# Attention products over 4, 32 or 64 keys made with 128 contraction rows in the second layer

## The chip, the cores and the metric

The kernel runs on one core of one Trainium2 chip. The metric is the device time of one launch in microseconds. Before the change it is 934.2 us, the median of three runs (933.96 to 939.34).

## What is computed

One inference step of a two-layer decoder, for a prompt of 512 tokens and for 8 sample sequences of 4 new tokens each. Layer one is a state-space mixer. After it, keys and values (8 heads of 128) are made once; layer two, where the change lies, is attention over them with three dilation groups per head:

```python
WINDOWS = (128, 512, 2048); DILATIONS = (1, 4, 16)
def dilated_mixer(h, attend, biases, g_norm, w_in, w_out):
    u = rmsnorm(h, g_norm) @ w_in                       # 24 query heads and a gate
    for g in range(N_DIL_GROUPS):
        o, lse = attend(q[:, :, g], biases[g], DILATIONS[g], WINDOWS[g] // DILATIONS[g])
        ...
    w = softmax(stack(lses)); o = sum(w * stack(outs))  # groups weighted by their log-sum-exp
    return (o * silu(gate)) @ w_out
```

A prompt query attends causally to prompt keys at distances 0, d, 2d, ...; a sample query attends to the same pattern over a cache of 1024 older rows followed by its own 4 new rows. In both, the weights p = exp(score - max) multiply the values.

## The kernel before

All weights of the projections are split into a high and a low part (`whi`, `wlo`), so that a projection is three products per block. In layer two one core does three things interleaved on TensorE:

- the projections of layer two (tiles `pa`, `pb`), which run as a "filler": after each attention step the program puts 24 or 20 projection matmuls into the stream;
- `attend(h, n)`, the prompt attention of head h and query block n (0 to 3, 128 queries each). Queries and keys are ordered by residue class mod 4. The scores `sp` are one dense product for the window of 128 and, for the strided groups, products per residue class r that give w = 32(n+1) keys. `ptp` holds the transposed weights, which ScalarE copies to `pt`. `pv` is the output: one or two products of 128 keys, and then four products, one for each r, of 32 output columns with w rows of weights against `vr`, the values in strided order. w is 32, 64, 96 and 128 for n = 0, 1, 2, 3;
- `sample(h, q)`, the sample attention of head h and half q (4 sequences each): scores `s1`, `s2` against 640 cached keys (`kc`) and the 4 new ones, weights transposed (`w`) and copied to `wt`, and the output `so`: five products of 128 keys (`vc`) for each of 4 sequences, and a sixth of 4 keys (`vn`, the new values).

The order on TensorE is that of the written program. A loop over units (four `attend` and two `sample` per head, 49 units with one `combine` that joins the groups of the samples) calls at each turn one stage of each unit in flight and then the filler. A unit's stages are scores, transposes, output product, and (for `attend`) the transpose of the output. Loads go through SyncE's queue in program order: `kc`, `vc` and `vn` per sample unit, `kv` (a head's keys, values and, in four blocks of 32 partitions, the strided values) once per head, `wraw` (projection weights). `kc` and `vc` have two buffers each, one for each half of a unit's load.

In the profile all matmuls are recorded at line 146 (`mm`), transposes at line 149; each f32 matmul of these attention tiles shows as two records. "128\*32" behind a tile's name is rows by columns of the weights in the array. Loading weights into the array is a row of its own (PEld).

Of the kernel before, what the change touches and what calls it, by code (L numbers as in the profile page):

```python
# [12 lines left out]
F32 = mybir.dt.float32  # L13
# [8 lines left out]
TS = 4  # L22
# [12 lines left out]
ATH = 8  # L35
# [92 lines left out]
def tile_yoco_step(  # L128
# [6 lines left out]
    nc = tc.nc  # L135
    dma = nc.sync.dma_start
# [8 lines left out]
    def mm(*a, **k):  # L145
        pin(nc.tensor.matmul(*a, **k))  # L146
# [144 lines left out]
    vnd = dram.tile([NB, TS, ATH, 128], F32, name="vnd")  # L291
    kvd = dram.tile([ATH, 128, T + SEQ], F32, name="kvd")

    def dap(t, off, ap):
        a = t[:]
        return bass.AP(tensor=a.tensor, offset=a.offset + off, ap=ap)
# [3 lines left out]
    wk = actx.enter_context(tc.tile_pool(name="wk_a", bufs=2))  # L300
# [645 lines left out]
    wk = bctx.enter_context(tc.tile_pool(name="wk_b", bufs=2))  # L946
# [90 lines left out]
    for m in range(KD):  # L1037
        w = nxt
# [61 lines left out]
    for i, (f, h, wi) in enumerate(order):  # L1100
        w = [nxt]
# [63 lines left out]
    wk = bctx.enter_context(tc.tile_pool(name="wk_d", bufs=2))  # L1165
# [8 lines left out]
    y_s = wk.tile([128, ATH, NB * TS], F32, name="ys", bufs=1)  # L1174
    qpad = [wk.tile([128, NB, 32], F32, name=f"qpad{i}", bufs=1) for i in range(3)]
    sbt = wk.tile([128, SK], F32, name="sbt", bufs=1)
    for t_ in qpad + [sbt]:
        nc.gpsimd.memset(t_, 0.0)
    scale = 1.0 / math.sqrt(128.0)
    qp_t, kv_t = {}, {}  # L1180
# [186 lines left out]
    def attend(h, n):  # L1367
        bt, qp = bt_t[h], [qp_t[h, g] for g in range(3)]
        kv = kv_t[h]
        kt = kv[:, 0, :]  # L1370
        vb, vr = (kv[:, i, 0:SEQ].rearrange("p (n d) -> p n d", n=4) for i in (1, 2))
        kp = kt[:, NS:T]
        ktr = kp.rearrange("p (n r i) -> p r n i", n=4, r=4)
        bt12 = bt[:, 256:512].rearrange("p (a c) -> p a c", a=2)
        w = 32 * (n + 1)
        g0 = 128 if n == 0 else 256
        sp = pss("sp")
        k0 = max(0, n - 1) * 128
        for g in range(2):
            for r in range(4):  # L1380
                mm(sp[32 * r:32 * r + 32, g0 + w * g:g0 + w * g + w],
                   qp[1 + g][:, 128 * n + 32 * r:128 * n + 32 * r + 32], ktr[:, r, 0:n + 1, :], start=True, stop=True)
        mm(sp[:, 0:g0], qp[0][:, 128 * n:128 * n + 128], kp[:, k0:128 * n + 128], start=True, stop=True)
        s_ = wk.tile([128, 512], F32, name="s", bufs=3)
        mx = wk.tile([128, 4], F32, name="mx", bufs=4)
        s12 = s_[:, g0:g0 + 2 * w].rearrange("p (a c) -> p a c", a=2)
        nc.vector.tensor_tensor_reduce(out=s12, in0=sp[:, g0:g0 + 2 * w].rearrange("p (a c) -> p a c", a=2),
                                       in1=bt12[:, :, 128 - w:128], scale=1.0, scalar=-3e38,
                                       op0=ALU.add, op1=ALU.max, accum_out=mx[:, 1:2])
        nc.vector.tensor_tensor_reduce(out=s_[:, 0:g0], in0=sp[:, 0:g0], in1=bt[:, 256 - g0:256], scale=1.0,  # L1390
                                       scalar=-3e38, op0=ALU.add, op1=ALU.max, accum_out=mx[:, 0:1])
        nc.vector.tensor_scalar(mx[:, 2:3], mx[:, 0:1], mx[:, 1:2], -1.0, op0=ALU.max, op1=ALU.mult)
        nc.scalar.activation(s_[:, 0:g0 + 2 * w], s_[:, 0:g0 + 2 * w], AF.Exp, bias=mx[:, 2:3], accum_out=mx[:, 3:4])
        nc.vector.tensor_tensor(s12[:, 0, :], s12[:, 0, :], s12[:, 1, :], op=ALU.add)
        nc.vector.reciprocal(mx[:, 3:4], mx[:, 3:4])
        yield
        tp = pss("ptp", (128, 3, 128))
        nk = g0 // 128
        for i in range(nk):
            transpose(tp[:, i, :], s_[:, 128 * i:128 * i + 128], ident)  # L1400
        transpose(tp[0:w, 2, :], s_[:, g0:g0 + w], ident)
        pt = wk.tile([128, 3, 128], F32, name="pt", bufs=2)
        nc.scalar.copy(pt[:, 0:nk, :], tp[:, 0:nk, :])
        nc.scalar.copy(pt[0:w, 2, :], tp[0:w, 2, :])
        yield
        pv = pss("pv")[:, 0:128]
        for i in range(nk):
            b = n - nk + 1 + i
            mm(pv, pt[:, i, :], vb[:, b, :], start=i == 0, stop=False, skip_group_check=True)
        for r in range(4):  # L1410
            mm(pv[32 * r:32 * r + 32, :], pt[0:w, 2, 32 * r:32 * r + 32], vr[0:w, r, :],
               start=False, stop=True, skip_group_check=True)
        on = wk.tile([128, 128], F32, name="on", bufs=1)
        nc.scalar.activation(on, pv, AF.Copy, scale=mx[:, 3:4])
        yield
        if h not in op_t:
            op_t[h] = pss("op")
        op = op_t[h]
        transpose(op[:, 128 * n:128 * n + 128], on, ident)
        op_n[h] = op_n.get(h, 0) + 1  # L1420
        yt = y_t[h // 4][:, h % 4, :]
        if h == 7 and op_n[h] >= 3:
            c0, c1 = ((128, SEQ), (0, 128))[op_n[h] - 3]
            y7 = yt[:, NS + c0:NS + c1]
            assert len(gated) == 2
            nc.vector.scalar_tensor_tensor(y7, op[:, c0:c1], 0.5, y7, op0=ALU.mult, op1=ALU.mult)
            y_split(h, NS + c0, NS + c1)
        elif h < 7 and op_n[h] == 4:
            nc.vector.tensor_copy(yt[:, NS:T], op)
            att_done.add(h)  # L1430
# [5 lines left out]
    def sample(h, q):  # L1436
        if q == 0:
            sample_bias(h)
        qs = qpad[h % 3]
        kt = kv_t[h][:, 0, :]  # L1440
        s1, s2 = pss("s1"), pss("s2")
        kc = []
        for jp in range(2):
            kc.append(wk.tile([128, 2, NU], F32, name="kc", bufs=2))
            dma(kc[jp], ck[h, q, :, 2 * jp:2 * jp + 2, :])

        for o, c0, c1 in ((s1, 0, 512), (s2, 512, NU), (s2, NU, SK)):
            for j in range(4):
                b = 4 * q + j
                keys = kc[j // 2][:, j % 2, c0:c1] if c1 <= NU else kt[:, TS * b:TS * b + TS]  # L1450
                mm(o[32 * j:32 * j + 32, c0 % 512:c0 % 512 + c1 - c0], qs[:, b, :], keys, start=True, stop=True)
        ss = wk.tile([128, SK], F32, name="ss", bufs=1)
        mx = wk.tile([128, 4], F32, name="mxs", bufs=2)
        i16 = 2 * h + q
        nc.vector.tensor_tensor_reduce(out=ss[:, 0:512], in0=s1, in1=sbt[:, 0:512], scale=1.0, scalar=-3e38,
                                       op0=ALU.add, op1=ALU.max, accum_out=mx[:, 0:1])
        nc.vector.tensor_tensor_reduce(out=ss[:, 512:SK], in0=s2[:, 0:SK - 512], in1=sbt[:, 512:SK], scale=1.0,
                                       scalar=-3e38, op0=ALU.add, op1=ALU.max, accum_out=mx[:, 1:2])
        nc.vector.tensor_scalar(mx[:, 2:3], mx[:, 0:1], mx[:, 1:2], -1.0, op0=ALU.max, op1=ALU.mult)
        nc.scalar.activation(ss, ss, AF.Exp, bias=mx[:, 2:3], accum_out=lsm[:, i16:i16 + 1])  # L1460
        nc.gpsimd.tensor_copy(lse[:, i16:i16 + 1], mx[:, 2:3])
        nc.vector.reciprocal(mx[:, 3:4], lsm[:, i16:i16 + 1])
        vc = []
        for jp in range(2):
            vc.append(wk.tile([128, 2, 5, 128], F32, name="vc", bufs=2))
            dma(vc[jp], cv[h, q, :, 2 * jp:2 * jp + 2, :, :])
        yield
        vn = wk.tile([TS, 4, 128], F32, name="vn", bufs=1)
        dma(vn, dap(vnd, h * 128 + 4 * q * TS * ATH * 128, [[ATH * 128, TS], [TS * ATH * 128, 4], [1, 128]]))
        w1, w2 = pss("w1", (128, 4, 128)), pss("w2", (128, 2, 128))  # L1470
        for i in range(5):
            transpose((w1[:, i, :] if i < 4 else w2[:, 0, :]), ss[:, 128 * i:128 * i + 128], ident)
        transpose(w2[0:TS, 1, :], ss[:, NU:SK], ident)
        wt = wk.tile([128, 6, 128], F32, name="wt", bufs=1)
        nc.scalar.copy(wt[:, 0:4, :], w1)
        nc.scalar.copy(wt[:, 4, :], w2[:, 0, :])
        nc.scalar.copy(wt[0:TS, 5, :], w2[0:TS, 1, :])
        yield
        so = pss("so")[:, 0:128]
        for i in range(6):  # L1480
            for j in range(4):
                rows = slice(32 * j, 32 * j + 32)
                if i < 5:
                    mm(so[rows, :], wt[:, i, rows], vc[j // 2][:, j % 2, i, :], start=i == 0, stop=False, skip_group_check=True)
                else:
                    mm(so[rows, :], wt[0:TS, 5, rows], vn[:, j, :], start=False, stop=True, skip_group_check=True)
        nc.scalar.activation(o_s[:, q, h, :], so, AF.Copy, scale=mx[:, 3:4])

    def combine():
# [161 lines left out]
    for u in range(len(units) + LA + 2):  # L1651
        i = u - LA
# [5 lines left out]
        if u < len(units):  # L1658
            f, a = units[u]
# [104 lines left out]
```

## Time and profile before

| | us |
|---|---|
| median of three runs | 934.2 |
| the profiled execution | 930.12 |
| its span, first to last instruction | 928.3 |
| TensorE busy in the span | 912.0 (98%) |
| VectorE / ScalarE / GpSimd busy | 683.7 / 489.6 / 163.9 |
| granted TensorE clock, mean | 0.998 |

"Busy" of TensorE counts the time in which a matmul is under way, and its matmuls overlap, so short pauses between their starts do not show as idle time; they show in the starts and in the idle time of the weight loads. Layer two's attention runs from about 590 to 870 us.

### The profile page before, as it was taken

What the parts mean: (1) busy time and instruction counts of PE and PEld (TensorE: products, weight loads), DVE (VectorE), ACT (ScalarE), POOL (GpSimd) and SP (SyncE); (2) the same over time, 40 slices, a digit from 0 to 9 for tenths busy, and PEclk for the clock granted to TensorE, in tenths of its full rate; (3) what the DMA queues carried; (4) which work ended last, traced back from release to release, by engine and by line L of the source; (5) the groups of instructions that cost most, each with busy time, mean ns of one, the idle gap of its engine ahead of it and who ended that gap; (6) DMA issues with size and microseconds to landing.
All of it is one profiled execution on the core that took longest, in us unless ns stands there. A gap on an engine that the chain in (4) does not pass through costs nothing.

```text
span 928.3 us, 21878 instructions
## 1 busy us (share of the span) xinstructions
PE 912.0 (98%) x8671; PEld 842.9 (91%) x8671; DVE 683.7 (74%) x1435; ACT 489.6 (53%) x1140; POOL 163.9 (18%) x206
## 2 busy tenths in 40 slices
PE   8999999999999999999999999999999999999997
PEld 8989888988788889999999999988888888888997
DVE  6998899989799799555598346866677766777732
ACT  6678655755665655322255213555555555557642
POOL 2030344533433533111011000000000000000021
PEclk9999999999999999999999999999999999999999
DMA  8224365365357432546286555767867877784511
GB/s 296 92 74 158 97 212 188 122 200 159 127 171 233 138 132 96 159 137 209 84 285 204 190 177 181 255 208 250 279 192 250 265 228 255 258 267 144 191 49 49
DMA packets 80573, 168.48 MB, mean 182 GB/s; under 512 B 19990, under 2 KB 37736, under 8 KB 79960
## 3 DMA queue, kind: packets, MB, share of 16 engines
q1 hardware_dynamic: 73784, 154.60, 50.8%
q10 hardware_dynamic: 5616, 9.75, 2.8%
q0 software_dynamic: 1072, 2.74, 1.2%
q8 instruction: 68, 1.11, 0.5%
q14 instruction: 33, 0.27, 0.1%
HBM read 141.14 MB, written 25.93 MB: 180 GB/s over the span
## 4 chain that ended last, share of the span: by engine, by line
PE 82%; DVE 10%; ACT 2%; DMA 2%; issue 2%; POOL 0%; SPq 0%; ACTq 0%; POOLq 0%; DVEq 0%
PE pa L146 33%; PE pb L146 28%; PE sp L146 3%; PE so L146 3%; PE pv L146 2%; PE s L146 2%; DVE wlo L206 2%; DVE co L641 1%; PE yd L146 1%; DVE vl L874 1%; DMA m<-aed 1%; PE w L149 1%; PE ptp L149 1%; PE csp L146 1%; PE xp L149 1%
## 5 line engine op out<-in xcount | busy, mean ns | idle before, releaser
L205 ACT ACTIVATE whi<-wraw 128x1024 fp32r<-128x1024 f32 x69 | 72.9, 1056 | 95.7 <-PE pb L146 53.0
L206 DVE TENSOR_TENSOR wlo<-wraw,whi 128x1024 fp32r<-128x1024 f32 x69 | 88.8, 1287 | 46.9 <-ACT whi L205 46.4
L146 PE MATMUL pa<-bq,whi 128*128 128x272 f32 x512 | 103.1, 296 | 0.0
L146 PE MATMUL pb<-nl,whi 128*128 128x288 f32 x280 | 83.6, 298 | 0.0
L146 PE MATMUL pb<-nh,wlo 128*128 128x288 f32 x280 | 83.1, 297 | 0.0
L146 PE MATMUL pb<-nh,whi 128*128 128x288 f32 x280 | 83.0, 296 | 0.0
L146 PEld LDWEIGHTS pa<-bq,whi 128*128 128x128 f32 x512 | 81.2, 189 | 0.9
L146 PE MATMUL pa<-nh,whi 128*128 128x256 f32 x280 | 80.0, 286 | 0.0
L146 PE MATMUL pa<-nl,whi 128*128 128x256 f32 x280 | 79.7, 285 | 0.0
L146 PE MATMUL pa<-nh,wlo 128*128 128x256 f32 x280 | 79.1, 282 | 0.0
L146 PE MATMUL pb<-bq,whi 128*128 128x272 f32 x384 | 77.2, 296 | 1.2 <-DVE kv L1225 0.8
L146 PE MATMUL pa<-bq,wlo 128*128 128x272 f32 x256 | 74.2, 290 | 0.0
L641 DVE SCALAR_TENSOR_TENSOR co<-cb,cvp,co 128x568 f32<-128x568 f32 x72 | 65.4, 911 | 1.3 <-ACT co L639 0.7
L146 PEld LDWEIGHTS pb<-bq,whi 128*128 128x128 f32 x384 | 60.8, 189 | 2.5 <-DVE kv L1225 1.0
L1284 ACT ACTIVATE whi<-wraw 128x512 fp32r<-128x512 f32 x64 | 40.1, 627 | 36.4 <-PE pb L146 16.6
L146 PEld LDWEIGHTS pb<-nl,whi 128*128 128x128 f32 x280 | 52.5, 188 | 4.4 <-issue 4.4
L146 PE MATMUL pb<-bq,wlo 128*128 128x272 f32 x192 | 55.4, 289 | 0.0
L146 PEld LDWEIGHTS pb<-nh,wlo 128*128 128x128 f32 x280 | 52.7, 188 | 2.2 <-issue 2.2
L146 PEld LDWEIGHTS pa<-nh,whi 128*128 128x128 f32 x280 | 52.8, 189 | 1.9 <-issue 1.9
L146 PEld LDWEIGHTS pa<-nl,whi 128*128 128x128 f32 x280 | 52.7, 188 | 1.4 <-issue 1.4
L146 PEld LDWEIGHTS pa<-nh,wlo 128*128 128x128 f32 x280 | 52.7, 188 | 0.9 <-issue 0.9
L146 PEld LDWEIGHTS pb<-nh,whi 128*128 128x128 f32 x280 | 52.6, 188 | 0.8 <-issue 0.8
(403 smaller groups left out, 2779.7 us busy)
## 6 DMA issues: line engine op xcount, KB each, us to landing
wraw<-w_in SPq DMA_DIRECT2D x40, 512.0 KB
kc<-ck SPq DMA_DIRECT2D x32, 640.0 KB
vc<-cv SPq DMA_DIRECT2D x32, 640.0 KB
wraw<-wb SPq DMA_DIRECT2D x32, 512.0 KB
s<-s SPq DMA_DIRECT2D x32, 256.0 KB
m<-aed SPq DMA_DIRECT2D x16, 512.0 KB
ssmS<-s ACTq DMA_DIRECT2D x32, 256.0 KB
wraw<-w_out SPq DMA_DIRECT2D x16, 512.0 KB
```

Source lines behind the costliest of these rows:

```text
L146: pin(nc.tensor.matmul(*a, **k))
L149: pin(nc.tensor.transpose(*a))
L205: a = nc.scalar.activation(hi, raw, AF.Copy)
L206: b = lo_eng.tensor_tensor(lo, raw, f32(hi), op=ALU.subtract)
L641: nc.vector.scalar_tensor_tensor(o, cb[:, k:k + n], cvp[:, ti, k:k + 1], o, op0=ALU.mult, op1=ALU.add)
L874: nc.vector.scalar_tensor_tensor(v_l[g][:, i, :], v_t[g][:, i, :], gg, f32(v_h[g][:, i, :]), op0=ALU.mult, op1=ALU.subtract)
L1284: nc.scalar.activation(hi, src[p][j], AF.Copy)
```

## The change

Three persistent tiles replace tiles that were allocated per unit: `ptz` (four, one for each n, for the strided weights that were the third block of `pt`), `wt` and `vn`. GpSimd zeroes `vn`, the sixth block of `wt` and the four `ptz` once, ahead of layer two's attention. ScalarE and the load write the same few rows as before, and the products read all 128 rows, so the rest multiplies by zero. For the strided products the values read are all 128 partitions of `vr`, and so all four blocks of `kv`'s third part instead of the first n+1.

```diff
-    for t_ in qpad + [sbt]:
+    ptz = [wk.tile([128, 128], F32, name=f"ptz{i}", bufs=1) for i in range(4)]
+    wt = wk.tile([128, 6, 128], F32, name="wt", bufs=1)
+    vn = wk.tile([128, 4, 128], F32, name="vn", bufs=1)
+    for t_ in qpad + [sbt, vn, wt[:, 5, :]] + ptz:
         nc.gpsimd.memset(t_, 0.0)
...
-        pt = wk.tile([128, 3, 128], F32, name="pt", bufs=2)
+        pt = wk.tile([128, 2, 128], F32, name="pt", bufs=2)
         nc.scalar.copy(pt[:, 0:nk, :], tp[:, 0:nk, :])
-        nc.scalar.copy(pt[0:w, 2, :], tp[0:w, 2, :])
+        nc.scalar.copy(ptz[n][0:w, :], tp[0:w, 2, :])
...
         for r in range(4):
-            mm(pv[32 * r:32 * r + 32, :], pt[0:w, 2, 32 * r:32 * r + 32], vr[0:w, r, :],
+            mm(pv[32 * r:32 * r + 32, :], ptz[n][:, 32 * r:32 * r + 32], vr[:, r, :],
                start=False, stop=True, skip_group_check=True)
...
-        vn = wk.tile([TS, 4, 128], F32, name="vn", bufs=1)
-        dma(vn, dap(vnd, ...))
+        dma(vn[0:TS], dap(vnd, ...))
...
-                if i < 5:
-                    mm(so[rows, :], wt[:, i, rows], vc[j // 2][:, j % 2, i, :], start=i == 0, stop=False, ...)
-                else:
-                    mm(so[rows, :], wt[0:TS, 5, rows], vn[:, j, :], start=False, stop=True, ...)
+                vals = vc[j // 2][:, j % 2, i, :] if i < 5 else vn[:, j, :]
+                mm(so[rows, :], wt[:, i, rows], vals, start=i == 0, stop=i == 5, ...)
```

No instruction changes its place on TensorE, VectorE, ScalarE or SyncE; what changes are shapes, and a few waits. On TensorE, the output product of head 2's block n = 0, before, with the strided products (32 output columns each) behind one of 128 keys, and the scores `sp` of the next unit behind them:

```order
L149 MATMUL w_8517<-ident,ss 4x128
L146 MATMUL pv<-kv,pt 128x128 [waits PE_49]
L146 MATMUL pv<-kv,pt 32x128 [waits DMAHW1_49]
L146 MATMUL pv<-kv,pt 32x128 x3
L146 MATMUL sp<-kv,qp 32x96 [waits DVE_49,PE_49]
L146 MATMUL sp<-kv,qp 32x96 x7
L146 MATMUL sp<-kv,qp 128x256
```

The same place of the changed kernel:

```order
L149 MATMUL w_8520<-ident,ss 4x128
L146 MATMUL pv<-kv,pt 128x128 [waits PE_49]
L146 MATMUL pv<-kv,ptz_7035 32x128 [waits DMAHW3_49,DMAHW4_49,DMAHW2_49,DMAHW1_49]
L146 MATMUL pv<-kv,ptz_7035 32x128 x3
L146 MATMUL sp<-kv,qp 32x96 [waits DVE_49,PE_49]
L146 MATMUL sp<-kv,qp 32x96 x7
L146 MATMUL sp<-kv,qp 128x256
```

The strided products now wait for four loads, one per block of 32 partitions, where they waited for one. On GpSimd, the zeroing ahead of layer two's attention, before (`lse<-mxs` is its next work, in the sample units):

```order
L1178 MEMSET qpad_7032 128x256
L1178 MEMSET qpad_7033 128x256
L1178 MEMSET sbt 128x644
L1461 COPY lse<-mxs 128x1 [waits DVE_49] x16
L1629 TENSOR_TENSOR e<-e 128x272 [waits PE_49,Activation_49]
```

and in the changed kernel:

```order
L1182 MEMSET qpad_7032 128x256
L1182 MEMSET qpad_7033 128x256
L1182 MEMSET sbt 128x644
L1182 MEMSET vn 128x512
L1182 MEMSET wt 128x128
L1182 MEMSET ptz_7035 128x128
L1182 MEMSET ptz_7036 128x128
L1182 MEMSET ptz_7037 128x128
L1182 MEMSET ptz_7038 128x128
L1465 COPY lse<-mxs 128x1 [waits DVE_49] x16
```

Six zeroings are added behind the four that stood there; the copies behind them are the same.

More of the change, by code (lines that the diff above doesn't have):

```diff
@@ L1467, in sample @@
         yield
-        vn = wk.tile([TS, 4, 128], F32, name="vn", bufs=1)
-        dma(vn, dap(vnd, h * 128 + 4 * q * TS * ATH * 128, [[ATH * 128, TS], [TS * ATH * 128, 4], [1, 128]]))
+        dma(vn[0:TS], dap(vnd, h * 128 + 4 * q * TS * ATH * 128, [[ATH * 128, TS], [TS * ATH * 128, 4], [1, 128]]))
         w1, w2 = pss("w1", (128, 4, 128)), pss("w2", (128, 2, 128))
@@ L1473, in sample @@
         transpose(w2[0:TS, 1, :], ss[:, NU:SK], ident)
-        wt = wk.tile([128, 6, 128], F32, name="wt", bufs=1)
         nc.scalar.copy(wt[:, 0:4, :], w1)
@@ L1482, in sample @@
                 rows = slice(32 * j, 32 * j + 32)
-                if i < 5:
-                    mm(so[rows, :], wt[:, i, rows], vc[j // 2][:, j % 2, i, :], start=i == 0, stop=False, skip_group_check=True)
-                else:
-                    mm(so[rows, :], wt[0:TS, 5, rows], vn[:, j, :], start=False, stop=True, skip_group_check=True)
+                vals = vc[j // 2][:, j % 2, i, :] if i < 5 else vn[:, j, :]
+                mm(so[rows, :], wt[:, i, rows], vals, start=i == 0, stop=i == 5, skip_group_check=True)
         nc.scalar.activation(o_s[:, q, h, :], so, AF.Copy, scale=mx[:, 3:4])
```

## The prediction

> **What bounds the kernel now.** I read the page's busy times and chain first, then three stretches by engine, then who waits for whom in the stretch of the change. From the page:
>
> ```profile
> PE 912.0 (98%) x8671; PEld 842.9 (91%) x8671; DVE 683.7 (74%) x1435; ACT 489.6 (53%) x1140; POOL 163.9 (18%) x206
> PE 82%; DVE 10%; ACT 2%; DMA 2%; issue 2%; POOL 0%; SPq 0%; ACTq 0%; POOLq 0%; DVEq 0%
> ```
>
> TensorE is 82% of the chain that ended last. The stretch from 590 to 860 us (busy us of TensorE, its weight loads, VectorE, ScalarE, GpSimd; clock, DMA share, GB/s), and the waits of TensorE and of its weight loads there (us in total, times, longest):
>
> ```profile
> 590.00:860.00 270.00, 269.25 (x3422) 236.14 (x3421) 193.84 (x602) 152.03 (x410) 4.59 (x16) 1.00 0.72 237
> PE pb L146 <- DVE kv L1225: 0.8, 1, 0.8
> PEld s L146 <- issue: 5.9, 22, 0.3
> PEld s L146 <- PE so L146: 5.4, 21, 0.3
> PEld sp L146 <- issue: 4.8, 24, 0.2
> PEld so L146 <- issue: 4.4, 23, 0.2
> PEld s L146 <- DMA kc<-ck: 1.3, 2, 0.7
> ```
>
> Of 270 us, TensorE's matmuls cover 269.25, and one wait, of 0.8 us, is put down to another engine; VectorE has 193.84 us of work there and ScalarE 152.03. The stretch is as long as TensorE's stream, so time taken out of that stream leaves the total unless something else is then late. But the weight loads pause: 4.4 us ahead of `so`, 4.8 ahead of `sp`, 11.3 ahead of `s`, nearly all in pauses of 0.2 to 0.3 us and most under "issue", where no engine is to be seen as the cause. These pauses decide what the change is worth.
>
> **Few rows are no shorter and no longer by themselves.** Groups by shape:
>
> ```profile
> L146 PE MATMUL so<-vc,wt 128*32 128x128 f32 x640 | 20.8, 275 | 0.0
> L146 PE MATMUL so<-vn,wt 4*32 4x128 f32 x128 | 6.7, 280 | 0.0
> L146 PE MATMUL pv<-kv,pt 96*32 96x128 f32 x64 | 3.4, 285 | 0.0
> L146 PE MATMUL pv<-kv,pt 64*32 64x128 f32 x64 | 3.4, 281 | 0.0
> L146 PE MATMUL pv<-kv,pt 32*32 32x128 f32 x64 | 3.4, 280 | 0.0
> ```
>
> A product with 4 rows takes 280 ns, one with 128 takes 275. What differs is when they start. The first sample's output, from four views of single moments and short windows (starts of the first instruction of each group):
>
> ```profile
> 606.46 0.51 PE L146 MATMUL so<-vc,wt 128*32 128x128 f32 x12
> ...
> 606.68 0.29 PE L146 MATMUL so<-vc,wt 128*32 128x128 f32 x3
> 606.90 0.42 PE L146 MATMUL so<-vn,wt 4*32 4x128 f32 x8
> 607.25 0.64 PE L146 MATMUL s<-kc,qpad 128*32 128x512 f32 x4
> ...
> 607.70 0.61 PE L146 MATMUL s<-kc,qpad 128*32 128x512 f32 x4
> 608.13 0.40 PE L146 MATMUL s<-kc,qpad 128*32 128x128 f32 x8
> ```
>
> Matmuls come in bursts of four, one for each group of 32 columns. In `so<-vc` the bursts at 606.46 (twelve records, three bursts) to 606.68 are (606.68 - 606.46)/2 = 0.11 apart. From the last of them to the 4-row group it is 0.22, its two bursts and the way out take 607.25 - 606.90 = 0.35, and the first step of the scores is 0.45 where the second is 0.43. Weight loads at the same kind of place, for the strided products of n = 0, n = 1 and n = 2:
>
> ```profile
> 702.24 0.57 PEld L146 LDWEIGHTS pv<-kv,pt 128*128 128x128 f32 x10
> 703.02 0.32 PEld L146 LDWEIGHTS sp<-kv,qp 128*32 128x32 f32 x16 [0.20 <-issue]
> ...
> 748.43 0.27 PEld L146 LDWEIGHTS sp<-kv,qp 128*32 128x32 f32 x12 [0.20 <-issue]
> ...
> 719.50 0.80 PEld L146 LDWEIGHTS pv<-kv,pt 128*128 128x128 f32 x12
> 720.29 0.64 PEld L146 LDWEIGHTS sp<-kv,qp 128*32 128x32 f32 x18
> ```
>
> Behind 32 rows (702 us) and 64 rows (748 us) the loads of `sp` pause 0.20 us; behind 96 rows (719 us) they do not. So the pause goes with row counts up to 64, on the way in (from 128 rows) and on the way out, and 96 rows count as 128. The Trainium skill, "TensorE: Matmul & The Clock Gate", section "Why this matters for your kernels", says that a single product over 32 rows takes the same time as one over 128; by that rule alone padding would be worth nothing. The durations here agree (280 against 275 ns), the starts do not (0.22 against 0.11 us).
>
> **The change part by part.** I take a step of a padded group to be as in `so<-vc`, 0.11 us.
>
> (1) `so`, 16 times. From 606.68 to 607.25 are three steps, 0.57 us; padded 3 x 0.11 = 0.33. Saved 0.24, and 0.02 at the scores' first step: 0.26. 16 x 0.26 = 4.2 us. Fourteen of the 16 are followed by scores `s`, two by `sp`, which I price alike. If the steps stayed at the 0.13 that a first step after a pause has (0.35 - 0.22), it would be 0.57 - 0.39 = 0.18, or 2.9 us.
>
> (2) `pv` of n = 0 and n = 1. The same scores (three key blocks) follow once 32 rows, once 128:
>
> ```profile
> 702.35 0.74 PE L146 MATMUL pv<-kv,pt 128*128 128x128 f32 x10
> 703.02 1.17 PE L146 MATMUL sp<-kv,qp 128*32 128x96 f32 x18
> 703.83 0.48 PE L146 MATMUL pa<-bq,whi 128*128 128x272 f32 x1
> ...
> 833.45 0.97 PE L146 MATMUL pv<-kv,pt 128*128 128x128 f32 x12
> 834.23 1.14 PE L146 MATMUL sp<-kv,qp 128*32 128x96 f32 x18
> 835.02 0.48 PE L146 MATMUL pb<-bq,whi 128*128 128x272 f32 x1
> ```
>
> 32 rows: 703.83 - 702.35 = 1.48 us. 128 rows: 1.57, but with two more records of 128 keys at 0.11 each, so 1.35 like for like. Saved 0.13 (0.11 at the way out alone: 0.67 - (0.78 - 0.22)). Eight blocks n = 1 and seven n = 0: 15 x 0.13 = 2.0 us, at least 15 x 0.11 = 1.7. The eighth n = 0 is the last unit; projections of full width follow it, I count nothing. n = 2 (96 rows) and n = 3 save nothing. The way in stays: from 128\*128 to 32 columns it is the same with 128 rows (the sum of the 833 us rows holds it).
>
> (3) Six zeroings on GpSimd:
>
> ```profile
> 570.42 0.81 POOL L1178 MEMSET qpad<- 128x256 f32 x3 [68.19 <-DVE wlo L1285]
> 571.17 0.64 POOL L1178 MEMSET sbt<- 128x644 f32 x1
> 593.77 0.19 POOL L1461 COPY lse<-mxs 128x1 f32<-128x1 f32 x1 [21.96 <-DVE mxs L1459]
> ```
>
> 644 columns take 0.64 us, so 512 + 5 x 128 = 1152 take about 1.2. GpSimd then idles 21.96 us; the first `vn` load is issued at 588 us, the first `wt` copy runs at 600. Nothing is charged; without that cover it would be 1.2 us once.
>
> (4) The wider reads wait for four `kv` loads instead of one or two at the head of n = 0 and n = 1. Where the lead is shortest, head 6:
>
> ```profile
> 771.83 3.15 SPq L1187 DMA_DIRECT2D kv<-kvd x4
> ...
> 803.45 0.74 PE L146 MATMUL pv<-kv,pt 128*128 128x128 f32 x10
> ```
>
> The last of the four is issued by 775.0, 28.5 us ahead. Nothing, from either side; a wait would queue the whole of TensorE behind it, since it works in order. Weight loads with 128 rows take some ns more (`so<-vc` 106 to 110 against 101 to 104) beside running matmuls: nothing.
>
> Sum: 4.2 + 2.0 = 6.2 us, with bounds 2.9 + 1.7 = 4.6 and, with the unrounded last digits upward (0.27 and 0.14), 6.4.
>
> **What is late next.** The cache loads `kc`. Twice, the scores stood for them:
>
> ```profile
> 651.84 0.83 SPq L1445 DMA_DIRECT2D kc<-ck x2
> ...
> 658.66 0.23 PEld L146 LDWEIGHTS s<-kc,qpad 128*32 128x32 f32 x7 [0.65 <-DMA kc<-ck]
> ...
> 718.84 0.83 SPq L1445 DMA_DIRECT2D kc<-ck x2
> ...
> 726.06 0.16 PEld L146 LDWEIGHTS s<-kc,qpad 128*32 128x32 f32 x8 [0.20 <-PE so L146]
> ```
>
> A lead of 657.87 - 651.84 = 6.0 us is too short, 7.2 us is enough. A round of one sample (some 17 us) shrinks by 0.26 + 0.13 = 0.4 us; a load whose issue does not move with TensorE loses as much lead. Six of 16 leads are between 5 and 7.5 us, so at most 6 x 0.4 = 2.4 us come back. Since the issues wait for buffers that TensorE frees, they move along with it, and I charge 0.3.
>
> **Rivals.**
>
> *The pause is not from the rows* (the change does not do what it is built on). For it: the wait list puts 21 pauses ahead of `s` down to `so`, as if the scores waited for that product to end; then those stay, and at the least nothing is saved: 934.2. Against: the same 0.20 stands ahead of `sp` behind 32 and 64 rows under "issue", and not behind 96.
>
> *Taken back by `kc`.* Gain 6.2 - 2.4 = 3.8: 930.4. For it the two waits above, against it that issues follow TensorE.
>
> *Slower: every score step waits for `kc`.* If leads fell under 6 us in all 16 samples and each cost the 0.7 us seen at worst, that is 16 x 0.7 - 1.3 = 9.9 us, more than the 6.2: 937.9. It decides where the leads, mostly 7 to 14 us, lose over a microsecond; 0.4 is not that.
>
> *The first steps stay slow*: the lower bound 4.6, so 929.6.
>
> **How the numbers follow.** The profiled execution took 930.12 us with a span of 928.3; the sum is made in its time, which is 4.1 under the median of the runs (934.2), and I take the difference off the median. Forecast 934.2 - 6.2 + 0.3 = 928.3. Chances: the forecast, within a microsecond and a half, 0.68; the slow first steps or `kc` in part (930 to 932) 0.18; no gain 0.08; `kc` everywhere 0.03; more than the sum 0.03. The range takes the upper bound of the sum and some 3 us of spread (934.2 - 6.4 - 2.8; single executions lie 4.1 under the median and 5.1 over it) and the partial cases: 925.0 to 932.5. One per cent, about what can be told from no change here, is 9.3 us: faster by that would be under 924.9, above every term, 0.05; slower 0.03; within 0.92.
>
> **What would show it.** Right: no pause of the loads between `so<-vc`, `so<-vn` and `s`; 0.33 us from the last `so<-vc` burst to the scores; `sp` behind n = 0 and 1 without a pause; 590 to 860 us of before done in some 264. Wrong: the pauses of 0.20 with 128 rows in every shape; more or longer waits of `s` for `kc`; the wait for `DVE kv` (0.8) grown by what TensorE gained; a new wait of `pv` for loads of `kv`.

## The result

The changed kernel takes 930.19 us, the median of six runs (928.57 to 931.42), against 934.71 us for the kernel before, measured beside it. The ratio is 0.9942, with a 95% interval of 0.992 to 0.9964: a gain of 4.5 us by the medians and of 5.4 by the ratio (3.4 to 7.5), clear of the spread and within one per cent. Forecast were 928.3 us, a gain of 5.9.

The page of the profile after, its busy times and chain; the stretch from 590 to 860 us; and the waits from 593 to 862 us:

```profile
PE 910.9 (98%) x8671; PEld 849.9 (92%) x8671; DVE 683.4 (74%) x1435; ACT 489.8 (53%) x1140; POOL 162.2 (17%) x212
PE 82%; DVE 9%; DMA 4%; ACT 3%; issue 2%; POOL 0%; SPq 0%; POOLq 0%; DVEq 0%; ACTq 0%
...
590.00:860.00 270.00, 267.78 (x3469) 242.85 (x3469) 196.73 (x614) 155.22 (x414) 4.59 (x16) 1.00 0.73 243
...
PE pb L146 <- DVE kv L1229: 1.1, 1, 1.1
PEld s L146 <- DMA kc<-ck: 2.4, 2, 1.5
PEld s L146 <- issue: 5.1, 17, 0.3
PEld s L146 <- PE so L146: 3.9, 13, 0.3
PEld sp L146 <- issue: 1.8, 9, 0.2
PEld so L146 <- issue: 1.6, 9, 0.2
```

Two things are to be seen. The short pauses of the weight loads shrank: `sp` from 4.8 to 1.8 us, `so` from 4.4 to 1.6, `s` from 11.3 to 9.0. Those left of `so` stand where the columns go from 128 to 32, those left of `sp` nearly all where they go back from 32 to 128, and those left of `s` between its own steps; the change touches none of these. And the waits grew: for `kc` from 1.3 to 2.4 us, for `DVE kv` (a tile that VectorE writes) from 0.8 to 1.1. The first sample's output, matmul starts and weight loads:

```profile
610.10 0.73 PE L146 MATMUL so<-vc,wt 128*32 128x128 f32 x20
610.64 0.40 PE L146 MATMUL so<-vn,wt 128*32 128x128 f32 x8
610.86 1.15 PE L146 MATMUL s<-kc,qpad 128*32 128x512 f32 x12
...
610.53 0.24 PEld L146 LDWEIGHTS so<-vn,wt 128*32 128x32 f32 x8
610.75 0.24 PEld L146 LDWEIGHTS s<-kc,qpad 128*32 128x32 f32 x8
...
704.45 0.16 PEld L146 LDWEIGHTS pv<-kv,ptz 128*32 128x32 f32 x8
704.59 0.73 PEld L146 LDWEIGHTS sp<-kv,qp 128*32 128x32 f32 x17
```

Twenty records of `so<-vc` (five bursts) take 0.54, so 0.11 each, and the two padded bursts 610.86 - 610.64 = 0.22 where they took 0.35; the loads run through without a pause, also from `pv` of n = 0 to `sp`. The durations of one product hardly changed (273 ns where the 4 rows took 280):

```profile
L146 PE MATMUL pv<-kv,ptz 128*32 128x128 f32 x256 | 13.6, 285 | 0.0
L146 PE MATMUL so<-vn,wt 128*32 128x128 f32 x128 | 6.4, 273 | 0.0
```

The spans of the two profiles, 928.3 and 928.1 us, do not show the gain, because single executions differ by several us ahead of the change. So I compare stretches. From the first scores to the first product of the joining of the samples (`oc`), before and after:

```profile
591.24 0.64 PE L146 MATMUL s<-kc,qpad 128*32 128x512 f32 x4
861.23 0.29 PE L146 MATMUL oc<-sbt,os 128*128 128x16 f32 x2
```

```profile
595.22 0.64 PE L146 MATMUL s<-kc,qpad 128*32 128x512 f32 x4
860.83 0.29 PE L146 MATMUL oc<-sbt,os 128*128 128x16 f32 x2
```

269.99 us became 265.61: 4.4 us, which agrees with the runs. The work ahead of the first scores, which is the same, took 4.0 us more in this execution; its granted clock was 0.98 and 0.99 in the first two stretches of 200 us, where it was 1.00 before. From 590 to 860 us it was 1.00 in both. What is left to explain is a forecast of 6.2 us taken out of TensorE's stream and 4.4 found.

### The profile page after: what moved, and what is told of

The parts are those of the page before. It is cut to its first block, busy times and chain, and to the rows that moved or that the text cites. A ratio compares the mean times of both kernels' runs of the same rounds, so it can differ in the third digit from the quotient of the medians.

```text
span 928.1 us, 21890 instructions
## 1 busy us (share of the span) xinstructions
PE 910.9 (98%) x8671; PEld 849.9 (92%) x8671; DVE 683.4 (74%) x1435; ACT 489.8 (53%) x1140; POOL 162.2 (17%) x212
## 4 chain that ended last, share of the span: by engine, by line
PE 82%; DVE 9%; DMA 4%; ACT 3%; issue 2%; POOL 0%; SPq 0%; POOLq 0%; DVEq 0%; ACTq 0%
PE pa L146 33%; PE pb L146 28%; PE sp L146 3%; PE so L146 2%; PE pv L146 2%; PE s L146 2%; DMA m<-aed 2%; DVE co L641 2%; DVE wlo L206 1%; PE yd L146 1%; PE csp L146 1%; PE w L149 1%; PE ptp L149 1%; PE xp L149 1%; DVE v L703 1%
```

## The experiments

### One part at a time

The first keeps the padding of the samples' new values and gives the strided products their 32, 64 and 96 rows back, the second the other way round.

```diff
-            mm(pv[...], ptz[n][:, 32 * r:32 * r + 32], vr[:, r, :], ...)
+            mm(pv[...], pt[0:w, 2, 32 * r:32 * r + 32], vr[0:w, r, :], ...)      # first
...
-                vals = vc[j // 2][:, j % 2, i, :] if i < 5 else vn[:, j, :]   # second
-                mm(so[rows, :], wt[:, i, rows], vals, ...)
+                if i < 5:
+                    mm(so[rows, :], wt[:, i, rows], vc[j // 2][:, j % 2, i, :], ...)
+                else:
+                    mm(so[rows, :], wt[0:TS, 5, rows], vn[0:TS, j, :], ...)
```

> The new values of the samples padded to 128 rows, the strided products left at 32, 64, 96 rows. Theory (TensorE pauses when its row count goes past 64 in either direction): the step from so<-vc to so<-vn falls from 202 to 89 ns and from there to the scores from 197 to 89, 16 times, while sp behind n = 0 and n = 1 still comes 197 to 199 ns late. About two thirds of the stream's gain, 16 x 0.27 = 4.3 us, before any waits for loads; total some 930 to 931. Rival (the pause ahead of the scores is a wait for so to end): that step stays at 197, gain at most 2.2 us.

> The strided products padded, the new values of the samples read with 4 rows again. Theory: sp behind n = 0 and n = 1 comes at 89 ns, so<-vn keeps its 202 and 197 ns; gain 15 x 0.13 = 2.0 us, total some 932 to 933. Rival (the padded products cost something of their own, or the wider reads wait for kv): gain near 0 or less, and a wait of pv for loads of kv in the trace.

Ratios to the kernel before: 0.9969 (0.9949 to 0.9989) for the new values alone, 0.9979 (0.996 to 0.9997) for the strided products alone; 931.58 and 932.37 us against 934.98. The first is a little above the 930 to 931 that was expected: its profile lists 3.4 us of waits for `kc`, and its stretch from the first scores to `oc` is only 1.5 us shorter than before (the second's, with 1.5 us of such waits, 1.9). Such figures do not separate 2 us from 4, but a part of the trace without these waits does. A head's two rounds, the second head's first scores to the third's, hold no wait but the constant ones; first the kernel before, then the changed one, then the two parts (each from a view of the 0.35 us around these starts):

```profile
624.17 0.64 PE L146 MATMUL s<-kc,qpad 128*32 128x512 f32 x4
657.87 0.62 PE L146 MATMUL s<-kc,qpad 128*32 128x512 f32 x2
```

```profile
627.39 0.61 PE L146 MATMUL s<-kc,qpad 128*32 128x512 f32 x4
660.27 0.60 PE L146 MATMUL s<-kc,qpad 128*32 128x512 f32 x2
```

```profile
627.13 0.61 PE L146 MATMUL s<-kc,qpad 128*32 128x512 f32 x4
660.28 0.60 PE L146 MATMUL s<-kc,qpad 128*32 128x512 f32 x2
```

```profile
628.14 0.64 PE L146 MATMUL s<-kc,qpad 128*32 128x512 f32 x4
661.59 0.62 PE L146 MATMUL s<-kc,qpad 128*32 128x512 f32 x2
```

33.70 us before, 32.88 after, 33.15 with the new values alone, 33.45 with the strided products alone. The new values save 0.55 per head, 0.27 a sample; the strided products 0.25, 0.13 a block; together 0.82. The fourth, fifth and sixth heads repeat the first two of these figures within 0.01 us. Both parts do what the forecast said, they add up (0.80 against 0.82), and the rival that the pause ahead of the scores is a wait for `so` to end is out: it went with the rows alone.

### Which row counts

The third kernel pads the new values to 64 rows (and leaves the strided products padded to 128), the fourth pads everything to 96.

```diff
-                vals = vc[j // 2][:, j % 2, i, :] if i < 5 else vn[:, j, :]
-                mm(so[rows, :], wt[:, i, rows], vals, ...)
+                r_ = 128 if i < 5 else 64      # third; fourth: 96, and ptz[n][0:max(w, 96)], vr[0:max(w, 96)]
+                vals = vc[j // 2][:, j % 2, i, :] if i < 5 else vn[0:r_, j, :]
+                mm(so[rows, :], wt[0:r_, i, rows], vals, ...)
```

> As the changed kernel, but the new values of the samples padded to 64 rows only. Theory (it is the class of the row count, 96 and 128 being one class, 32 and 64 others): the two steps are 202 and 197 ns again, the stream 16 x 0.27 = 4.3 us longer than with 128 rows. Rival (4 rows are special, or padding helps by itself, or the new place of vn and wt in memory does it): the steps stay at 89 ns and the time at that of the changed kernel.

> As the changed kernel, but all padding goes to 96 rows instead of 128 (new values, and the strided products of n = 0 and n = 1). Theory: 96 counts as 128, every step at 89 ns, the time that of the changed kernel within the runs' spread. Rival (only equal row counts run through without a pause): steps of about 200 ns at so<-vn and behind pv, some 6 us more than the changed kernel.

With 64 rows, the head and its way out:

```profile
626.49 0.42 PE L146 MATMUL so<-vn,wt 64*32 64x128 f32 x8
626.85 0.64 PE L146 MATMUL s<-kc,qpad 128*32 128x512 f32 x4
660.29 0.62 PE L146 MATMUL s<-kc,qpad 128*32 128x512 f32 x2
```

With 96:

```profile
627.88 0.40 PE L146 MATMUL so<-vn,wt 96*32 96x128 f32 x8
628.10 0.61 PE L146 MATMUL s<-kc,qpad 128*32 128x512 f32 x4
661.00 0.60 PE L146 MATMUL s<-kc,qpad 128*32 128x512 f32 x2
```

64 rows give 0.36 from group to scores and a head of 33.44 us, as if the new values had 4 rows (33.45); 96 rows give 0.22 and 32.90, as 128 does (32.88). The ratios lean the same way, though their intervals overlap: 0.9978 (0.9962 to 0.9995) and 0.9955 (0.9938 to 0.9973). The zeroed tiles and their place in memory are the same in both, so they are not it. The Trainium skill, "TensorEngine Tiling (Array Packing)", section "Key Properties", says that a change of tiling mode drains the engine; its section "Available Configurations" names modes of 32, 64 and 128 rows. The runs agree as far as they go: they show no drain as such, only later starts, some 0.11 us at each crossing between 64 rows or fewer and 96 or more, and with the slower step behind it 0.13 to 0.15 in all. A crossing between 32 and 64 rows was not tried.

### One crossing instead of two

Four rows again, but as the first of the six products: `for i in (5, 0, 1, 2, 3, 4)`, with `start` and `stop` moved.

> As the changed kernel, but the new values of the samples have 4 rows again and come first of the six products instead of last. The way from the transposes to 32 columns costs 202 ns in any case, so theory: the 4-row group follows the transposes at 202, the first so<-vc follows it at about 197, and the scores follow the last so<-vc at 89; one pause instead of two, so the stream is 16 x 0.13 = 2.1 us longer than in the changed kernel. Rival (4-row products cost by themselves, wherever they stand): both steps about 200 ns, 4.3 us longer.

```profile
627.92 0.61 PE L146 MATMUL s<-kc,qpad 128*32 128x512 f32 x4
661.09 0.60 PE L146 MATMUL s<-kc,qpad 128*32 128x512 f32 x2
```

33.17 us a head, 0.29 more than in the changed kernel: 0.15 a sample, one crossing where 4 rows at the end cost two (0.27). Expected was 0.13. The ratio is 0.9949 (0.9934 to 0.9965), not to be told from the changed kernel: it had fewer waits for `kc` (1.3 us in four). So the cost is not in the four-row products themselves but in where they stand.

### Where the rest of the gain went: loads of cached keys

In the changed kernel the weight loads of the scores stand here:

```profile
661.27 0.23 PEld L146 LDWEIGHTS s<-kc,qpad 128*32 128x32 f32 x7 [0.88 <-DMA kc<-ck]
...
820.99 0.17 PEld L146 LDWEIGHTS s<-kc,qpad 128*32 128x32 f32 x4 [0.80 <-PE pv L146]
822.68 0.16 PEld L146 LDWEIGHTS s<-kc,qpad 128*32 128x32 f32 x8 [1.51 <-DMA kc<-ck]
```

The first and third are the places that waited before, by 0.65 and 0.67 us; the pause of 0.80, which the profile puts down to another product, and the 1.51 behind it are one unit, head 7's first. The loads of its keys were issued here, before and after, and between them those of head 2 after (heads count from 0):

```profile
814.75 2.38 SPq L1445 DMA_DIRECT2D kc<-ck  x2
...
654.59 0.83 SPq L1449 DMA_DIRECT2D kc<-ck  x2
...
814.32 2.58 SPq L1449 DMA_DIRECT2D kc<-ck  x2
```

Counted from each execution's first scores (591.24 and 595.22), head 2's loads were issued 1.2 us earlier than before, its scores began 1.6 us earlier. Head 7's loads were issued 4.4 us earlier, but TensorE was there 5.3 us earlier (at 820.19, where the pause of 0.80 begins, against 821.53 before). So the leads, from issue to scores, fell from 6.0 to 5.7 us and from 6.8 to 5.9: the issues moved along only in part. At head 7 they waited for other things than TensorE: the bias loads ahead of them 1.8 us for VectorE in both kernels, and the second load of keys 1.6 us for a load of values before and 1.8 after.

I tried to take these waits away twice by issuing the loads earlier. One kernel loads the next unit's keys right behind this unit's values:

```diff
+        nxt = (h, 1) if q == 0 else (h + 1, 0)      # behind the loads of vc
+        if nxt[0] < ATH:
+            kc_t[nxt] = load_kc(*nxt)
```

> The changed kernel, to be compared with the next on one chip: 0.994 of the kernel before, 929 to 931 us; two score steps wait for kc, some 2 to 2.5 us together, from 593 to 862 us.

> As the changed kernel, but the cached keys of the next sample unit are loaded right behind the cached values of this one, a round earlier in SyncE's queue (same buffers, same bytes). Theory (the rest of the stream's gain goes into waits for kc that is issued too late): no wait of s for kc, 2 us off the changed kernel, total 0.992 of the kernel before, stretch from the first scores to the last output product 6.2 us or more shorter than before. Rival (the queue's bandwidth, not the time of issue, sets when the data are there): waits of the same 2 us or more move to other loads (vc, wraw) and the time stays or grows.

The changed kernel again: 0.9953 (0.9935 to 0.997), with 2.4 us of waits for `kc`, as expected. The other: 1.0157 (1.0139 to 1.0175), 949.38 us, where 0.992 was expected. No score waited for `kc`, so the first half of the theory held; the second failed by 20 us. Its waits of weight loads, and of SyncE's queue:

```profile
PEld ptp L149 <- ACT s L1397: 10.7, 5, 4.3
...
SPq L1446 <- PE s L146: 14.8, 14, 4.9
SPq L1365 <- DMA kc<-ck: 9.0, 6, 2.7
```

SyncE's queue issues the loads in the order of the program: the early loads wait 14.8 us for their buffers (`PE s`), and the bias loads behind them wait for `kc` in turn, with the weights' loads behind those. TensorE then waits for the softmax on ScalarE. Why the softmax is late stays open: VectorE's waits for projection weights are no longer than in the changed kernel (1.7 us against 1.9). Not all of the 20 us are waits. Behind the longest, 4.04 us up to 852.97, the granted clock was 0.50 from 852 to 858 us, and 0.50 again at 774 to 776 behind one of 2.07; by its means of 0.83 (770 to 780) and 0.66 (850 to 860), at most some 5 us, an estimate, went there.

The milder version moves only the keys of a head's first unit, ahead of four small loads of the bias, in the changed kernel and in the kernel before:

```diff
-        if q == 0:
-            sample_bias(h)          # four loads of 30 KB that wait for VectorE
         ... # the two loads of kc
+        if q == 0:
+            sample_bias(h)
```

> The changed kernel with one change of order in SyncE's queue: in the first sample unit of each head, the two loads of cached keys come before the four small ones of the bias (which wait for VectorE to have read the bias of the head before) instead of behind them. Both score steps that waited were such units. Theory (kc is issued too late at these two places, and the queue has room there: DMA share 0.28 two us ahead of one of them): the waits of s for kc, 2.4 us in all, go, the weights' loads are not moved as in the kernel that loads kc a round early, so 1.5 to 2.4 us off the changed kernel, 0.991 to 0.993 of the kernel before. Rival (what is saved ahead of the scores is lost behind them, since the bias then comes late for VectorE): VectorE waits for sbt, and the time stays within 0.5 us or grows.

> The same change of order in the kernel before. Theory: its two waits for kc (1.3 us) go, so 0.998 to 0.999 of the kernel before; and the changed kernel with this order is then shorter by the whole of what was taken out of TensorE's stream, 6.0 to 6.4 us from the first scores to the last output product of the samples. Rival (the loss of the changed kernel lies elsewhere): the two differ by no more than the 4.3 us that the kernels without it do.

1.0013 (0.9995 to 1.0032) and 1.0054 (1.0037 to 1.0072): 935.48 and 940.13 us, worse by some 5 in both, where a gain of 1 to 2.4 us was expected. So moving the issue ahead is no cure. In the changed kernel with this order one wait for `kc` was left, of 1.4 us at another unit; in the kernel before there was none. New waits came in their place:

```profile
718.26 0.69 DVE L1265 TENSOR_TENSOR sums<-wraw 128x512 f32<-128x512 f32 x1 [2.27 <-DMA wraw<-wb]
...
DVE sums L1265 <- DMA wraw<-wb: 6.6, 4, 3.3
PEld sp L146 <- ACT wt L1477: 2.0, 1, 2.0
PEld ptp L149 <- DVE s L1398: 1.8, 1, 1.8
```

VectorE stood 2.27 us for projection weights, 6.6 in all (1.9 in the changed kernel), with the softmax queued behind; TensorE's weight loads then stood for `wt` and for the softmax, as they did not in the changed kernel. That the weights came late because the keys went ahead of them is argued from the order, not shown. The stretch of the changed kernel with this order was 5.7 us shorter than that of the kernel before with it (270.55 against 276.25), less than the 6.0 expected. The pair does not settle it: the waits differ, and in the second the granted clock was 0.83 from 840 to 850 us, 1.00 in the first.

So the last pair takes the load away instead of moving it: the first unit's keys serve all units, and 15 of 16 loads of 1.3 MB are left out.

> The changed kernel with the cached keys loaded once, by the first sample unit, and used by all 16 (15 of 16 loads of 1.3 MB each are left out, and so the scores of the other units are of other keys). Theory (the part of the gain that is missing was taken back by these loads, which share a nearly full queue): no wait of s for kc; against the next kernel, the stretch from the first scores to the joining of the samples is 6.0 to 6.4 us shorter, all that left TensorE's stream. Rival (the missing part is in TensorE's own stream or in VectorE and ScalarE): the two differ by some 4.4 us as the full kernels do.

> The kernel before with the cached keys loaded once (15 of 16 loads left out, scores of the other units of other keys). Theory: rounds of one head 33.70 us as in the kernel before, 1 to 1.5 us less than before in all, since its waits for kc go; some 6.2 us longer than the changed kernel under the same cut. Rival: some 4.4 us longer.

First scores and first `oc` under this cut, the kernel before and the changed one, and their stretches by engine:

```profile
594.42 0.64 PE L146 MATMUL s<-kc,qpad 128*32 128x512 f32 x4
862.68 0.29 PE L146 MATMUL oc<-sbt,os 128*128 128x16 f32 x2
...
590.00:860.00 270.00, 270.00 (x3457) 237.59 (x3456) 195.99 (x609) 152.60 (x409) 4.59 (x16) 1.00 0.52 167
```

```profile
598.65 0.64 PE L146 MATMUL s<-kc,qpad 128*32 128x512 f32 x4
860.84 0.29 PE L146 MATMUL oc<-sbt,os 128*128 128x16 f32 x2
...
590.00:860.00 270.00, 268.94 (x3497) 245.61 (x3496) 200.79 (x621) 156.40 (x416) 4.60 (x16) 1.00 0.55 174
```

268.26 us against 262.19: 6.1 shorter, and with the 0.3 by which the wait for `DVE kv` grew (0.8 to 1.1 here too), 6.4 left TensorE's stream. Neither kernel waits for `kc`; the share of the DMA engines is 0.52 and 0.55 instead of 0.72 and 0.73. In the full kernels the loads of keys cost 269.99 - 268.26 = 1.7 us before and 265.61 - 262.19 = 3.4 after. The difference, 1.7, is the missing gain: 6.1 - 1.7 = 4.4. Heads without a wait take 33.70 and 32.88 or 32.89 us in these two kernels as in the full ones, so the pairs can be compared; but each stretch is one execution, and the changed kernel's second one was 265.23, which would make it 1.3. End to end the two take 932.55 and 926.73 us, ratios 0.9967 (0.9946 to 0.9988) and 0.9903 (0.9873 to 0.9933).

## Why the prediction was right, and where it was off

- *The number*: 930.2 lies in the range, but not within the microsecond and a half of 928.3 that had 0.68; it is the case of "`kc` in part" (930 to 932, 0.18), and nearest to it is the rival *Taken back by `kc`* (930.4).
- *What bounds*: right. TensorE's stream decided, 82% of the chain before and after.
- *The pause comes from the row count, with 96 rows as 128*: right, shown by 4, 64, 96 and 128 rows in one place. The rival of equal durations (no gain) fell with it, as did the wait for `so`.
- *Term 1*, the new values: 0.26 forecast, 0.27 measured, 16 times. *Term 2*, the strided products: 0.13 and 0.13. The sum of 6.2 compares with 6.4 (6.1 by the stretches without the loads, 0.3 for `DVE kv`); the bound of slow first steps did not come true.
- *Nothing for the zeroings and the wider reads*: right. GpSimd's six zeroings are over by 577 us and its next work starts at 598; no wait of `pv` for `kv` appears:

```profile
575.73 0.53 POOL L1182 MEMSET vn<- 128x512 f32 x1
...
576.34 0.65 POOL L1182 MEMSET ptz<- 128x128 f32 x4
597.76 0.19 POOL L1465 COPY lse<-mxs 128x1 f32<-128x1 f32 x1 [20.77 <-DVE mxs L1463]
```

- *What is late next*: the right transfer, the wrong size. Charged were 0.3 us, on the reason that the issues move along with TensorE; measured were 1.7, inside the bound of 2.4 that the rival priced. That reason is the step that failed: the issues came 1.2 us earlier where TensorE came 1.6 (head 2), and 4.4 where it came 5.3 (head 7, where they waited for VectorE and for a load of values). The leads shrank by 0.35 and 0.9 us, the waits grew by 0.2 and 1.6; at head 7 the second load also took 0.5 us longer (816.55 to 822.68, against 816.77 to 822.44), for which no cause is shown. Nor does the lead alone decide, as I had read it: before the change, head 7's first unit waited with a lead of 6.8 us, and head 6's second, with 6.5 (803.75 to 810.24), did not; head 7's second load was issued 2.0 us behind its first. How full the DMA engines were does not tell it alone either: their share was 0.96 to 1.04 from 814 to 820 us, ahead of head 7's wait, but 0.28 to 0.78 from 652 to 660, ahead of head 2's. The wait for `DVE kv`, named among the dangers, took 0.3 more. What fixes how much comes back in one execution (2.4 us of waits in one kernel and 3.2 in another with the same stream, that of 96 rows) stays open.
- *The slower rival* (all 16 units wait) did not come; two or three units did.

## What to carry to other kernels

In this kernel products over few rows are not free when they stand between products over many: each crossing between 64 rows or fewer and 96 or more costs TensorE 0.11 to 0.15 us, which shows not in any instruction's duration but in the starts and in pauses of the weight loads, most of them under "issue". Zero rows cost nothing that these traces show; putting the small product next to a crossing that is paid anyway saves nearly half without zeros. Before charging a saving in full, find the loads with the shortest leads and what their issue waits for: here a quarter of 6 us came back as waits for loads, where issues had not followed TensorE, and moving loads ahead cost more than it saved.

## What the runs showed that I had not expected

The way from 128\*128 to 32 columns, and the way back, keep their pause of 0.2 us whatever the rows (what is left of `so` and `sp` under "issue"). TensorE's longer waits can cost twice: behind a wait of 4.04 us its granted clock stood at 0.50 for some 6 us. Issuing one load a round earlier, with the same buffers and bytes, made the kernel 20 us slower than the changed one (949.38 against 929.86 us), and taking the keys' loads ahead of the bias loads in one queue cost 5 us: the order of loads in this stretch is worth more than the whole change.
